# Loading a decayed cumulative sum's first operands by hardware queues as float32 rows, with GpSimd's queue begun later

## The chip, the cores and the metric

The kernel runs on one core of one Trainium2 chip. The metric is device time in microseconds (us). Each version is run several times; one further execution is profiled. Times inside that execution are counted from the start of its span.

The engines are TensorE (PE; PEld is its loading of weights), VectorE (DVE), ScalarE (ACT), GpSimd (POOL) and SyncE (SP). SP, ScalarE and GpSimd can issue DMAs. DMAs issued by SP and ScalarE go through hardware queues, those of GpSimd through a software queue, which alone converts float32 to bfloat16 on the way in this kernel.

## What is computed

```python
B, S, D = 16, 2048, 1024          # x: [B, S, D], w: [D, D], decay: [D], all float32
xw = x @ w
out[:, 0, :] = xw[:, 0, :]
for t in range(1, S):
    out[:, t, :] = decay * out[:, t - 1, :] + xw[:, t, :]
```

## The kernel before, in words

The 16 sequences are cut into 64 chunks of 512 time steps (TL). Chunks go in pairs, so one slot of the main loop is one pair and one of K = 8 blocks n of 128 output columns. For a slot, TensorE runs 8 contraction blocks k for each of the two chunks: 16 matmuls of 128x512, in bfloat16, into PSUM (`matmul`, line 125; the instruction is at line 131). VectorE scans along time, ScalarE copies and scales, GpSimd adds, VectorE transposes back, SP stores.

In the steady state x comes through GpSimd's queue as bfloat16 (`load`, line 101; issued at line 105), VectorE transposes it in 32x32 blocks (`turn`, 115) and ScalarE regroups it into xt (`part`, 123).

The order is written out by hand. `pin` keeps each instruction in program order on its engine, and `agenda` (line 571) is a list of deeds by slot: a letter names a function in `deeds` (line 524), the number is its argument. The list under -99 is the start, before the first slot, and it is the one that changes. Each engine runs its own instructions of that list in order, so a deed that waits holds back every later one on its engine.

What the start has to bring in:

- w comes in four quarters, named (h, e): h is the half of the output columns, e the parity of k. Contraction blocks k = 2m + e, m = 0 to 3, so the quarter (0, 0) holds the even k and (0, 1) the odd k for the first four blocks n. Each quarter is four DMAs, one for each group ("quad") of 32 partitions. `load_w` (321, issued at 323) brings them into `stage`, `settle` (328, copy at 330) rearranges a block of a quarter into `wsb`, which the matmuls read. `settle_slots` (416, copy at 419) does it for some n only: `q4` and `Q4` are the first slot and the others of the block k = 1.
- x's chunk 0 is wanted in two halves of 256 time steps. The first half comes as rows, 128 time steps to a DMA, by SP and ScalarE (line 341), as float32. `gather` (374, copy at 376; deeds H on VectorE, J on ScalarE) casts and regroups it into `upright`, TensorE transposes it against `eye` (`erect`, 383; line 386; deed t) into PSUM (`bed`), and `lay` (389, copy at 393; deeds o on VectorE, O on ScalarE) copies it into xt.
- Chunk 0's second half and chunk 1 come through GpSimd's queue (M1, M2, M3), and VectorE's block transposes (E) and copies (F on VectorE, G on ScalarE) lay them into xt.

TensorE's start is, in order: 12 spins (`spin`, 350; matmuls over zeros, line 352), the transposes t0 to t3, nine spins gated by the landing of w's first quarter (K; `spin_on`, 403, with a small copy on ScalarE at 404), n0 (`begin`, 395: the 16 matmuls over even k of chunk 0's first half, 256 columns each), n1 (the same for its second half), and then, in slot 0 (line 677), the 16 matmuls of 512 columns over the odd k of the whole chunk, followed by chunk 1. These read w's second quarter, settled by q4, w5, Q4, W6 and W7. From there on TensorE goes on into the slots.

GpSimd's start is, in order: U0 (w's first quarter), I1 (`eye`, lines 442 and 443), M1 (x's second half), U1 (w's second quarter), M2 and M3 (chunk 1), U2 and U3 (w's other two quarters).

Of the kernel before, what the change touches and what calls it, by code (L numbers as in the profile page):

```python
# [9 lines left out]
FP32 = mybir.dt.float32  # L10
BF16 = mybir.dt.bfloat16
# [3 lines left out]
def _ap(ap_obj: bass.AP, new_ap, extra_offset=0):  # L15
    return dataclasses.replace(
        ap_obj,
        ap=[list(p) for p in new_ap],
        offset=ap_obj.offset + extra_offset,
    )  # L20
# [5 lines left out]
def kernel(  # L26
# [26 lines left out]
    nc = tc.nc  # L53
    pin = tc.keep_in_program_order
    B, S, D = x.shape
    assert w.shape == (D, D)

    NQ = 4
    P = 32
    CQ = D // NQ  # L60
    K = CQ // P
    M = K // 2
    TL = 512
    NJ = TL // P
# [5 lines left out]
    const = ctx.enter_context(tc.tile_pool(name="const", bufs=1))  # L70
    sb = ctx.enter_context(tc.tile_pool(name="sb", bufs=1))
# [4 lines left out]
    def ring(pool, name, count, shape, dtype=FP32):  # L76
        i = turns[name] = turns.get(name, -1) + 1
        return pool.tile(shape, dtype, name=f"{name}{i % count}")

    def quad(q):  # L80
        return slice(q * P, (q + 1) * P)
# [12 lines left out]
    def ot_tile(nj):  # L94
        return ring(sb, "ot", 4, [128, nj, CR])

    xb_of = {}
    xw_of = {}
    xt_of = {}
# [25 lines left out]
    def matmul(ps, n, k, xt, t0=0, t1=TL, start=0, pairs=None):  # L125
        if pairs is None:
            rhs = xt[:, k // 2, k % 2, t0:t1]
        else:
            rhs = pairs[:, k // 2, t0 // P:t1 // P, :, k % 2].rearrange("p j i -> p (j i)")
        lhs = wsb[:, k, n].rearrange("p q i -> p (q i)")  # L130
        pin(nc.tensor.matmul(  # L131
            out=ps[:, t0:t1] if ps.shape[1] >= t1 else ps,
            lhsT=lhs,
            rhs=rhs,
            start=(k == 0 and t0 == start),
            stop=(k == K - 1),
        ))
# [3 lines left out]
    class Tile:  # L141
# [39 lines left out]
        def copy(self):  # L181
            self.xs = sb.tile([128, 2 * TL], FP32, name=f"xs{self.lot % 3}")[:, 0:self.T]
            parts = self.ps if isinstance(self.ps, tuple) else (self.ps,)
            size = self.T // len(parts)
            for i, ps in enumerate(parts):
                pin(nc.scalar.copy(out=self.xs[:, i * size:(i + 1) * size], in_=ps))  # L186
# [103 lines left out]
    class Outlet:  # L290
# [8 lines left out]
        def store(self, b, t0, j0, j1):  # L299
# [4 lines left out]
            for j in range(j0, j1, nj):  # L304
# [8 lines left out]

    room = [ot_tile(2 * NJ).rearrange("p j c -> p (j c)") for _ in range(2)]
    size = M * CH
    stage = {(0, 0): room[0][:, 0:size // 2].bitcast(BF16),
             (0, 1): room[0][:, size:size * 3 // 2].bitcast(BF16),
             (1, 0): room[1][:, 0:size // 2].bitcast(BF16),
             (1, 1): room[1][:, size // 2:size].bitcast(BF16)}

    def load_w(queues, h, e):
        for i, q in enumerate((0, 2, 1, 3)):
            pin(queues[i % len(queues)].dma_start(  # L323
                out=stage[h, e][quad(q)].rearrange("p (m d) -> p m d", m=M),
                in_=_ap(w, [[2 * D, P], [2 * P * D, M], [1, CH]],
                        (q * CQ + e) * D + h * CH)))
# [6 lines left out]
    idle = const.tile([128, TL], BF16, name="idle")  # L333
    spare = ring(psp, "spare", 1, [128, TL])
    rows = const.tile([128, 2, P], FP32, name="rows")
    touch = const.tile([128, 1], BF16, name="touch")
    H = NJ // 2
    halves = ((0, H), (H, NJ))
    whole = room[1][:, size:2 * size].rearrange("p (u c) -> p u c", u=2)
    for u, queue in enumerate((nc.sync, nc.scalar)):  # L340
        pin(queue.dma_start(out=whole[:, u], in_=_ap(x, [[D, 128], [1, D]], u * 128 * D)))
    pin(nc.vector.memset(idle, 0.0))  # L342
    pin(nc.vector.memset(rows, 0.0))
    pin(nc.scalar.copy(out=touch, in_=idle[:, 0:1]))

    gates = [const.tile([128, 128], BF16, name=f"gate{q}") for q in range(NQ)]
    for gate in gates:
        pin(nc.vector.memset(gate, 0.0))

    def spin(count, by):  # L350
        for _ in range(count):
            pin(nc.tensor.matmul(out=spare, lhsT=by, rhs=idle, start=True, stop=True))  # L352

    spin(12, idle[:, 0:128])
    for q in range(NQ):
        pin(nc.sync.dma_start(
            out=rows[q * P:q * P + R],
            in_=_ap(decay, [[P, R], [CH, 2], [1, P]], q * CR)))
    cols = const.tile([128, 2, P], FP32, name="cols")

    def load_half(i):
# [5 lines left out]
    firsts = [ps[:, 0:TL] for ps in heads] + [spares[0]]  # L367
    seconds = [ps[:, TL:2 * TL] for ps in heads] + [spares[1]]
    eye = const.tile([128, 128], BF16, name="eye")

    upright = room[0][:, size * 3 // 2:2 * size].bitcast(BF16).rearrange(
        "p (e u m c) -> p e u m c", e=2, u=2, m=M)

    def gather(i, copy):
        e, u = i // 2, i % 2
        pin(copy(out=upright[:, e, u].rearrange("p m (q i) -> p m q i", q=NQ),
                 in_=whole[:, u].rearrange(
                     "p (q m i e) -> p e m q i", q=NQ, m=M, e=2)[:, e]))

    def bed(e):  # L380
        return seconds[e].bitcast(BF16).rearrange("p (m t) -> p m t", m=M)

    def erect(i):
        e, u = i // 2, i % 2
        for m in range(M):
            pin(nc.tensor.transpose(
                out=bed(e)[:, m, u * 128:(u + 1) * 128], in_=upright[:, e, u, m], identity=eye))

    def lay(i, copy):
        e, m = i // 2, i % 2 * 2  # L390
        if 0 not in xt_of:
            xt_of[0] = ring(sb, "xt", 5, [128, M, 2, TL], BF16)
        pin(copy(out=xt_of[0][:, m:m + 2, e, 0:H * P], in_=bed(e)[:, m:m + 2]))

    def begin(i):
        for k in range(0, K, 2):
            for n in range(R):
                if i == 0:
                    matmul(firsts[n], n, k, xt_of[0], 0, H * P)
                else:  # L400
                    matmul(firsts[n], n, k, xt_of[0], H * P, TL, pairs=xw_of[0])

    def spin_on(q):
        pin(nc.scalar.copy(out=gates[q][quad(q), 0:1], in_=stage[0, 0][quad(q), 0:1]))
        spin(3 if q == 0 else 2, gates[q])

    def load_part(i):
        load_w((nc.gpsimd,), i // 2, i % 2)

    def part_one(i, copy):  # L410
        part(i // 8, copy, i % 4, i % 4 + 1, *halves[i // 4 % 2])
# [106 lines left out]
    def turn_and_load(c):  # L518
# [16 lines left out]
        "w": lambda i: settle_one(i, nc.scalar.copy),  # L535
        "M": load_half,
        "U": load_part,
        "E": lambda i: turn(i // 8, *halves[i // 4 % 2], i % 4, i % 4 + 1),
        "F": lambda i: part_one(i, nc.vector.tensor_copy),
        "G": lambda i: part_one(i, nc.scalar.copy),  # L540
        "K": spin_on,
        "t": erect,
        "H": lambda i: gather(i, nc.vector.tensor_copy),
        "J": lambda i: gather(i, nc.scalar.copy),
        "O": lambda i: lay(i, nc.scalar.copy),
        "o": lambda i: lay(i, nc.vector.tensor_copy),
        "n": begin,
        "q": lambda i: settle_slots(i, 0, 1),
        "Q": lambda i: settle_slots(i, 1, R),
# [19 lines left out]
        "L": lambda i: load(*loads.pop(0)) if loads else None,  # L569
    }  # L570
    agenda = {
# [92 lines left out]
    for step, (g, n) in enumerate(slots):  # L664
        T = TL * len(g)
        left = step - len(slots)
        if n % R == 0:
            ns, nj = range(n, n + R), T // P
            if left == -2 * R:
                outlets = [Outlet(ns, H, half) for half in range(2)]  # L670
            else:
# [4 lines left out]
        if step == 0:  # L676
# [3 lines left out]
            for k0 in range(0, K, 2):  # L680
                for i in range(R):
                    for k in (k0, k0 + 1):
                        matmul(seconds[i], i, k, xt_of[1], 0, H * P,
                               pairs=xw_of[1] if k0 < 4 else None)
            for i in range(R):
                for k in range(K):
                    matmul(seconds[i], i, k, xt_of[1], H * P, TL, H * P,
                           pairs=xw_of[1] if i < 2 else None)
        if step < R:
            ps = heads[n] if n < 3 else tuple(spares)  # L690
        else:
# [16 lines left out]
            elif step == K:  # L708
                todo = []
                nexts = (ring(psp, "spare", 1, [128, TL]), ring(psp, "ps", 3, [128, TL]))  # L710
                for l in range(len(g)):
                    for i, half in enumerate((ps[:, l * TL:(l + 1) * TL], nexts[l])):
                        for k in range(K):
                            matmul(half, n + i, k, xt_of.get(g[l]),
                                   pairs=xw_of[g[l]] if g[l] in (3,) else None)
# [51 lines left out]
```

## Time and profile before

| what | value |
|---|---|
| median of 3 runs | 903.76 us (903.57 to 903.91) |
| profiled execution: device time | 903.72 us |
| profiled execution: span | 901.9 us |
| granted clock of TensorE, mean | 1.00 |
| TensorE busy in matmuls | 891.2 us, 99% of the span |
| VectorE, ScalarE, GpSimd busy | 91%, 76%, 73% |
| chain that ended last, share on TensorE | 97% |
| w's DMAs, 16 of 128 KB, issue to landing, median | 5.6 us |
| x's first half, two DMAs of 512 KB, issue to landing | 4.7 and 4.9 us |

The span is the time from the first to the last instruction of the profiled execution; the device time is 1.8 us longer. Busy time is a mean over the whole span. The change lies in the first 15 us, so the views that matter are the timelines of the engines there and the chain of waits, not the shares. In a line of a timeline the first number is the start in us, the second the length of the group, then come engine, line, operation, output and input, the count, and in brackets the idle time just before it and what ended it.

### The profile page before, as it was taken

To read this page: it belongs to the slowest core of one execution; us is meant where nothing else is said; L and a number is where in the kernel's file an instruction comes from. 1 tells how busy PE (TensorE), PEld (TensorE's weight loads), DVE (VectorE), ACT (ScalarE), POOL (GpSimd) and SP (SyncE) were. 2 spreads that over 40 slices of the span, in tenths; PEclk is the share of its full clock that TensorE was granted. 3 is DMA by queue.
4 is the path that set the end of the run, shared out by engine and by line. 5 is a ranking of instruction groups with operands and counts; after the bars stand their busy time and mean duration, and the time that the engine had idled before them with its cause. 6 is when DMAs were issued, how large, how long until landed. Compare 5 with 4: busy or idle time off the path is not lost.

```text
span 901.9 us, 12229 instructions
## 1 busy us (share of the span) xinstructions
PE 891.2 (99%) x4131; PEld 411.9 (46%) x4213; DVE 823.5 (91%) x636; ACT 687.1 (76%) x962; POOL 657.2 (73%) x757
## 2 busy tenths in 40 slices
PE   8999999999999999999999999999999999999998
PEld 5544444444444444444444444444444444444444
DVE  4999998989999999999998999999999999999998
ACT  4889867778877877878778778777787787787743
POOL 8888678768767768677677687777777776876532
PEclk9999999999999999999999999999999999999999
DMA  9999999999999999999999999999999999999868
GB/s 193 195 215 218 229 212 207 216 233 247 247 248 255 248 255 252 246 254 250 222 235 228 218 236 227 233 226 227 232 230 227 227 236 222 226 228 221 177 153 231
DMA packets 402382, 204.77 MB, mean 227 GB/s; under 512 B 9360, under 2 KB 401552, under 8 KB 402320
## 3 DMA queue, kind: packets, MB, share of 16 engines
q1 hardware_dynamic: 265664, 134.77, 60.8%
q0 software_dynamic: 136512, 68.70, 56.8%
q8 instruction: 33, 0.54, 0.2%
q10 hardware_dynamic: 144, 0.52, 0.1%
q14 instruction: 29, 0.24, 0.1%
HBM read 138.42 MB, written 134.22 MB: 302 GB/s over the span
## 4 chain that ended last, share of the span: by engine, by line
PE 97%; DMA 1%; issue 1%; POOL 0%; DVE 0%; ACT 0%; DVEq 0%; POOLq 0%
PE ps L131 96%; PE spare L131 1%; DMA ot<-in_w_dram 1%; POOL ot L323 0%; DVE so L233 0%; PE ps L460 0%; PE spare L460 0%; ACT xb L467 0%; DVE wsb L419 0%; DVEq L419 0%; POOLq L751 0%
## 5 line engine op out<-in xcount | busy, mean ns | idle before, releaser
L131 PE MATMUL ps<-xt,wsb 128*128 128x512 bf16 (+1 forms) x3946 | 862.6, 378 | 4.7 <-DVE wsb L419 0.4
L131 PEld LDWEIGHTS <-wsb 128*128 128x128 bf16 x4160 | 406.5, 98 | 479.8 <-issue 0.9
L208 POOL TENSOR_TENSOR xs<-h,xs 128x512 f32<-128x512 f32 (+1 forms) x190 | 242.7, 1278 | 184.1 <-ACT h L169 83.1
L283 DVE STREAM_TRANSPOSE ot<-so 128x1024 f32<-128x1024 f32 (+2 forms) x265 | 300.2, 1171 | 6.5 <-DMA out_dram<-ot 4.4
L186 ACT COPY xs<-ps 128x1024 f32<-128x1024 f32 (+1 forms) x190 | 188.8, 994 | 149.3 <-PE ps L131 137.5
L266 POOL TENSOR_TENSOR so<-h,xs 128x512 f32<-128x512 f32 (+1 forms) x190 | 241.2, 1271 | 46.9 <-ACT h L169 27.2
L123 ACT COPY xt<-xw 128x2048 bf16<-128x2048 bf16 (+1 forms) x133 | 240.6, 1816 | 9.5 <-DVE xw L115 9.5
L105 POOL DMA_DIRECT2D xb<-in_x_dram x260 | 171.6, 661 | 2.9 <-DMA ot<-in_w_dram 0.9
L169 ACT ACTIVATE h<-so,dec 128x512 f32<-128x512 f32 (+1 forms) x190 | 145.3, 766 | 32.8 <-DVE so L213 29.9
L115 DVE STREAM_TRANSPOSE xw<-xb 128x2048 f32<-128x2048 f32 (+1 forms) x74 | 145.9, 1981 | 6.5 <-DMA xb<-in_x_dram 6.5
L213 DVE TENSOR_TENSOR_SCAN so<-spare,keep,xs 128x512 f32<-128x512 f32 (+1 forms) x97 | 119.8, 1237 | 25.9 <-POOL xs L208 25.6
L213 DVE TENSOR_TENSOR_SCAN so<-spare,xs 128x512 f32<-128x512 f32 x93 | 113.0, 1217 | 25.4 <-POOL xs L208 22.8
L169 ACT ACTIVATE h<-ps,dec 128x512 f32<-128x512 f32 (+1 forms) x189 | 129.3, 684 | 0.0
L233 DVE TENSOR_TENSOR_SCAN so<-dec,ps 128x1024 f32<-128x1024 f32 x34 | 76.9, 2260 | 0.8 <-ACT h L169 0.6
L233 DVE TENSOR_TENSOR_SCAN so<-dec,keep,ps 128x1024 f32<-128x1024 f32 (+2 forms) x35 | 74.7, 2138 | 0.0
L270 ACT COPY keep<-so 128x1 f32<-128x1 f32 x136 | 25.2, 188 | 9.1 <-DVE so L233 8.7
L204 ACT COPY so<-keep 128x1 f32<-128x1 f32 x97 | 18.4, 191 | 2.6 <-DVE ot L283 2.4
L131 PE MATMUL spare<-xt,wsb 128*128 128x512 bf16 (+1 forms) x68 | 14.0, 329 | 0.0
L323 POOL DMA_DIRECT2D ot<-in_w_dram x16 | 9.0, 561 | 2.9 <-POOLq L751 0.9
L202 POOL MEMSET so<- 128x1 f32 x93 | 10.7, 116 | 0.6 <-DVE ot L283 0.6
L131 PE MATMUL ps<-xw,wsb 128*128 128x256 bf16 (+1 forms) x56 | 9.3, 307 | 0.8 <-DVE xw L115 0.8
L352 PE MATMUL spare<-idle 128*128 128x512 bf16 x12 | 5.3, 632 | 1.2 <-DVE idle L342 1.2
(46 smaller groups left out, 43.9 us busy)
## 6 DMA issues: line engine op xcount, KB each, us to landing
out_dram<-ot SPq DMA_DIRECT2D x236, 512.0 KB, 10.8
xb<-in_x_dram POOLq DMA_DIRECT2D x248, 256.0 KB, 7.8
out_dram<-ot SPq DMA_DIRECT2D x56, 128.0 KB, 2.5
ot<-in_w_dram POOLq DMA_DIRECT2D x16, 128.0 KB, 5.6
out_dram<-ot SPq DMA_DIRECT2D x8, 256.0 KB, 4.2
xb<-in_x_dram POOLq DMA_DIRECT2D x12, 128.0 KB, 5.3
out_dram<-xb SPq DMA_DIRECT2D x4, 256.0 KB
ot<-in_x_dram ACTq DMA_DIRECT2D x1, 512.0 KB, 4.9
```

The source lines that it names most:

```text
L105: pin(nc.gpsimd.dma_start(out=xb_of[c][quad(q), j0:j1], in_=_ap(x, [[D, P], [P * D, j1 - j0], [1, CQ]], (b * S + t0 + j0 * P) * D + q * CQ)))
L115: pin(nc.vector.transpose(out=dst.rearrange("p (m j i) -> p j m i", m=M, i=P)[:, j0:j1, m0:m1], in_=src.rearrange("p (j m c) -> p j m c", ...
L123: pin(copy(out=xt_of[c][:, m0:m1, :, j0 * P:j1 * P], in_=src))
L131: pin(nc.tensor.matmul(out=ps[:, t0:t1] if ps.shape[1] >= t1 else ps, lhsT=lhs, rhs=rhs, start=(k == 0 and t0 == start), stop=(k == K - 1),))
L169: pin(nc.scalar.activation(out=h, in_=src, func=mybir.ActivationFunctionType.Copy, scale=dec[:, self.n:self.n + 1]))
L186: pin(nc.scalar.copy(out=self.xs[:, i * size:(i + 1) * size], in_=ps))
L208: pin(nc.gpsimd.tensor_tensor(out=odds, in0=self.g, in1=odds, op=ALU.add))
L213: pin(nc.vector.tensor_tensor_scan(out=so[:, 3:T + 2:2], data0=squares[-1][:, n:n + 1].to_broadcast([128, T // 2]), data1=self.xs[:, 1:T:2 ...
L233: pin(nc.vector.tensor_tensor_scan(out=so[:, t + 2:t + 2 + size], data0=dec[:, n:n + 1].to_broadcast([128, size]), data1=ps, initial=befor ...
L266: pin(nc.gpsimd.tensor_tensor(out=self.so[:, 2:T + 2:2], in0=self.h, in1=self.xs[:, 0:T:2], op=ALU.add))
L270: pin(nc.scalar.copy(out=self.keep, in_=self.so[:, self.T + 1:self.T + 2]))
L283: pin(nc.vector.transpose(out=outlet.ot[:, j:j + size, c0:c0 + P], in_=self.so[:, t1:t1 + size * P].rearrange("p (i t) -> p i t", t=P)))
```

## The change

It rewrites the start alone; everything from slot 0 on stays as it is.

- w's first quarter is loaded as float32 by SP (quads 0 and 1) and ScalarE (quads 2 and 3), behind x's first half on the same two queues. Its room in `stage` doubles, and `upright` moves into chunk 0's buffer of xw, which is not needed otherwise any more. `settle` of this quarter casts from float32 now.
- x's second half comes as rows too, one DMA on SP and one on ScalarE behind w's first quarter, into the buffer of xb that chunk 0 used. It takes the road of the first half: gathers H4, J5, H6, J7, transposes t4 to t7, copies o4, O5, o6, O7. The DVE transposes E4 to E7 and the copies G4, G5, F6, G7 go. `begin` is cut in four: n0 and n1 are the first half with k = 0, 2 and k = 4, 6; n2 and n3 the second half.
- GpSimd's queue begins with w's second quarter (U1). Ahead of it stands a new deed `v` (`hold`), a copy of two columns of x's first half, which waits until that has landed. U0 and M1 are gone.
- The four gates, their memsets and their copies on ScalarE go; K7 is seven spins without a gate, and m3 three spins into another bank, behind n1.
- Of w's first quarter VectorE settles blocks 0 and 1 and ScalarE blocks 2 and 3 (before: VectorE 0, 1 and 3, ScalarE 2).

```diff
--- before.py
+++ after.py
@@ -313,14 +313,14 @@
 
     room = [ot_tile(2 * NJ).rearrange("p j c -> p (j c)") for _ in range(2)]
     size = M * CH
-    stage = {(0, 0): room[0][:, 0:size // 2].bitcast(BF16),
+    stage = {(0, 0): room[0][:, 0:size],
              (0, 1): room[0][:, size:size * 3 // 2].bitcast(BF16),
              (1, 0): room[1][:, 0:size // 2].bitcast(BF16),
              (1, 1): room[1][:, size // 2:size].bitcast(BF16)}
 
-    def load_w(queues, h, e):
-        for i, q in enumerate((0, 2, 1, 3)):
-            pin(queues[i % len(queues)].dma_start(
+    def load_w(queue, h, e, quads):
+        for q in quads:
+            pin(queue.dma_start(
                 out=stage[h, e][quad(q)].rearrange("p (m d) -> p m d", m=M),
                 in_=_ap(w, [[2 * D, P], [2 * P * D, M], [1, CH]],
                         (q * CQ + e) * D + h * CH)))
@@ -334,24 +334,35 @@
     spare = ring(psp, "spare", 1, [128, TL])
     rows = const.tile([128, 2, P], FP32, name="rows")
     touch = const.tile([128, 1], BF16, name="touch")
+    held = const.tile([128, 2], FP32, name="held")
     H = NJ // 2
     halves = ((0, H), (H, NJ))
-    whole = room[1][:, size:2 * size].rearrange("p (u c) -> p u c", u=2)
-    for u, queue in enumerate((nc.sync, nc.scalar)):
-        pin(queue.dma_start(out=whole[:, u], in_=_ap(x, [[D, 128], [1, D]], u * 128 * D)))
+    xb_of[0] = ring(sb, "xb", 3, [128, NJ, CQ], BF16)
+    xw_of[0] = ring(sb, "xw", 2, [128, M, NJ, P, 2], BF16)
+    wholes = [room[1][:, size:2 * size],
+              xb_of[0].rearrange("p j c -> p (j c)").bitcast(FP32)]
+    wholes = [half.rearrange("p (u c) -> p u c", u=2) for half in wholes]
+
+    def load_rows(queue, i, u):
+        pin(queue.dma_start(
+            out=wholes[i][:, u], in_=_ap(x, [[D, 128], [1, D]], (2 * i + u) * 128 * D)))
+
+    load_rows(nc.sync, 0, 0)
+    load_rows(nc.scalar, 0, 1)
+    load_w(nc.sync, 0, 0, (0, 1))
+    load_w(nc.scalar, 0, 0, (2, 3))
+    load_rows(nc.sync, 1, 0)
+    load_rows(nc.scalar, 1, 1)
     pin(nc.vector.memset(idle, 0.0))
     pin(nc.vector.memset(rows, 0.0))
     pin(nc.scalar.copy(out=touch, in_=idle[:, 0:1]))
 
-    gates = [const.tile([128, 128], BF16, name=f"gate{q}") for q in range(NQ)]
-    for gate in gates:
-        pin(nc.vector.memset(gate, 0.0))
-
-    def spin(count, by):
+    def spin(count, into=spare):
         for _ in range(count):
-            pin(nc.tensor.matmul(out=spare, lhsT=by, rhs=idle, start=True, stop=True))
-
-    spin(12, idle[:, 0:128])
+            pin(nc.tensor.matmul(
+                out=into, lhsT=idle[:, 0:128], rhs=idle, start=True, stop=True))
+
+    spin(12)
     for q in range(NQ):
         pin(nc.sync.dma_start(
             out=rows[q * P:q * P + R],
@@ -368,44 +379,43 @@
     seconds = [ps[:, TL:2 * TL] for ps in heads] + [spares[1]]
     eye = const.tile([128, 128], BF16, name="eye")
 
-    upright = room[0][:, size * 3 // 2:2 * size].bitcast(BF16).rearrange(
-        "p (e u m c) -> p e u m c", e=2, u=2, m=M)
+    upright = xw_of[0].rearrange("p m j i e -> p (m j i e)").rearrange(
+        "p (h e u m c) -> p h e u m c", h=2, e=2, u=2, m=M)
 
     def gather(i, copy):
-        e, u = i // 2, i % 2
-        pin(copy(out=upright[:, e, u].rearrange("p m (q i) -> p m q i", q=NQ),
-                 in_=whole[:, u].rearrange(
+        h, e, u = i // 4, i // 2 % 2, i % 2
+        pin(copy(out=upright[:, h, e, u].rearrange("p m (q i) -> p m q i", q=NQ),
+                 in_=wholes[h][:, u].rearrange(
                      "p (q m i e) -> p e m q i", q=NQ, m=M, e=2)[:, e]))
 
-    def bed(e):
-        return seconds[e].bitcast(BF16).rearrange("p (m t) -> p m t", m=M)
+    def bed(h, e):
+        return seconds[2 * h + e].bitcast(BF16).rearrange("p (m t) -> p m t", m=M)
 
     def erect(i):
-        e, u = i // 2, i % 2
+        h, e, u = i // 4, i // 2 % 2, i % 2
         for m in range(M):
             pin(nc.tensor.transpose(
-                out=bed(e)[:, m, u * 128:(u + 1) * 128], in_=upright[:, e, u, m], identity=eye))
+                out=bed(h, e)[:, m, u * 128:(u + 1) * 128],
+                in_=upright[:, h, e, u, m], identity=eye))
 
     def lay(i, copy):
-        e, m = i // 2, i % 2 * 2
+        h, e, m = i // 4, i // 2 % 2, i % 2 * 2
         if 0 not in xt_of:
             xt_of[0] = ring(sb, "xt", 5, [128, M, 2, TL], BF16)
-        pin(copy(out=xt_of[0][:, m:m + 2, e, 0:H * P], in_=bed(e)[:, m:m + 2]))
+        pin(copy(out=xt_of[0][:, m:m + 2, e, h * H * P:(h + 1) * H * P],
+                 in_=bed(h, e)[:, m:m + 2]))
 
     def begin(i):
-        for k in range(0, K, 2):
+        h, k0 = i // 2, i % 2 * M
+        for k in (k0, k0 + 2):
             for n in range(R):
-                if i == 0:
-                    matmul(firsts[n], n, k, xt_of[0], 0, H * P)
-                else:
-                    matmul(firsts[n], n, k, xt_of[0], H * P, TL, pairs=xw_of[0])
-
-    def spin_on(q):
-        pin(nc.scalar.copy(out=gates[q][quad(q), 0:1], in_=stage[0, 0][quad(q), 0:1]))
-        spin(3 if q == 0 else 2, gates[q])
+                matmul(firsts[n], n, k, xt_of[0], h * H * P, (h + 1) * H * P)
+
+    def hold(i):
+        pin(nc.gpsimd.tensor_copy(out=held, in_=wholes[0][:, :, 0:1].rearrange("p u c -> p (u c)")))
 
     def load_part(i):
-        load_w((nc.gpsimd,), i // 2, i % 2)
+        load_w(nc.gpsimd, i // 2, i % 2, (0, 2, 1, 3))
 
     def part_one(i, copy):
         part(i // 8, copy, i % 4, i % 4 + 1, *halves[i // 4 % 2])
@@ -538,7 +548,9 @@
         "E": lambda i: turn(i // 8, *halves[i // 4 % 2], i % 4, i % 4 + 1),
         "F": lambda i: part_one(i, nc.vector.tensor_copy),
         "G": lambda i: part_one(i, nc.scalar.copy),
-        "K": spin_on,
+        "K": spin,
+        "m": lambda i: spin(i, seconds[0]),
+        "v": hold,
         "t": erect,
         "H": lambda i: gather(i, nc.vector.tensor_copy),
         "J": lambda i: gather(i, nc.scalar.copy),
@@ -569,7 +581,7 @@
         "L": lambda i: load(*loads.pop(0)) if loads else None,
     }
     agenda = {
-        -99: "U0 I1 M1 U1 M2 M3 U2 U3 H0 J1 t0 t1 H2 J3 t2 t3 O1 o0 K0 O3 o2 K2 K1 K3 W0 W1 w2 W3 n0 E4 E5 G4 E6 G5 E7 F6 G7 n1 q4 w5 Q4 W6 W7 D E8 E9 G8 E10 G9 E11 F10 G11 E12 L E13 G12 L E14 G13 E15 L F14 G15",
+        -99: "I1 v U1 M2 M3 U2 U3 H0 J1 t0 t1 H2 J3 t2 t3 O1 o0 O3 o2 K7 W0 w2 W1 w3 n0 n1 H4 J5 m3 H6 J7 t4 t5 o4 O5 n2 t6 t7 o6 O7 n3 q4 w5 Q4 W6 W7 D E8 E9 G8 E10 G9 E11 F10 G11 E12 L E13 G12 L E14 G13 E15 L F14 G15",
```

## The prediction, made before the changed kernel ran

> **What bounds the kernel now.** I read the waits of TensorE first, then the chain that ended last, then the timeline of each engine over the first 30 us, then the DMA queues in the same stretch. Waits of TensorE from 15 us to 898 us:
>
> ```profile
> engine line waited for: us in total, times, longest us
> PE ps L131 <- DVE wsb L419: 0.4, 1, 0.4
> ```
>
> That one wait ends at 14.97 us. Behind it TensorE never waits for another engine until the tail near 897 us, so the span is the moment T1 at which the matmuls over odd k of chunk 0 begin, plus a fixed run of matmuls: 901.9 - 14.97 = 886.9 us, with nothing in it that the change touches. An edit is worth what it does to T1, as long as what comes behind T1 is still fed. The chain of waits from 0 to 30 us says who sets T1 (start, length, what):
>
> ```profile
> 1.31 1.25 POOL ot L323 x2
> 2.56 5.65 DMA ot<-in_w_dram
> ...
> 9.16 5.43 DMA ot<-in_w_dram
> ...
> 14.72 0.21 DVE wsb L419
> ...
> 14.97 0.39 PE ps L131
> ```
>
> The last piece of w's second quarter is issued at 9.16 and lands at 14.60; VectorE copies a slot of it (0.21) and TensorE starts. T1 is bound by GpSimd's queue, whose third issue of that quarter had waited for a landing at 8.21. The timeline of TensorE shows what stands ahead of T1:
>
> ```profile
> 1.20 5.30 PE L352 MATMUL spare<-idle 128*128 128x512 bf16 x12 [1.20 <-DVE idle L342]
> 6.29 1.34 PE L386 MATMUL ps<-eye,ot 128*128 128x128 bf16 x16
> 7.95 2.16 PE L352 MATMUL spare<-idle,gate 128*128 128x512 bf16 x9 [0.32 <-ACT gate L404]
> ...
> 12.62 0.51 PE L131 MATMUL ps<-xw,wsb 128*128 128x256 bf16 x3 [0.76 <-DVE xw L115]
> ...
> 14.97 0.82 PE L131 MATMUL ps<-xt,wsb 128*128 128x512 bf16 x2 [0.37 <-DVE wsb L419]
> ```
>
> The 12 opening spins start 0.43 us apart; the spins from 7.95 start 0.22 apart: until about 7.0 us the array runs at half its later pace (the granted clock reads 1.00 in each of these stages; the spacing of the starts tells it). The second half of x is waited for at 12.62 (0.76 idle). The copies between, from the timelines of VectorE and ScalarE:
>
> ```profile
> 7.84 0.98 DVE L393 COPY xt<-ps 128x512 bf16<-128x512 bf16 x2 [1.62 <-ACT xt L393]
> 9.00 0.70 DVE L330 COPY wsb<-ot 128x512 bf16<-128x512 bf16 x3 [0.17 <-DMA ot<-in_w_dram]
> ```
>
> **The change, part by part.** Times are in this profiled execution (span 901.9, device time 903.72, 0.04 under the median of 903.76).
>
> *Loads.* w's first quarter goes as 1.05 MB of float32 (before: 0.52 MB, cast by GpSimd's queue), and x's second half as 1.05 MB of rows, both behind x's first half on the SP and ScalarE queues. The DMA queues over the first 5 us (packets, MB, share):
>
> ```profile
> q1 hardware_dynamic: 143, 0.52, 34.5%
> q10 hardware_dynamic: 133, 0.52, 26.7%
> q0 software_dynamic: 7, 0.01, 1.3%
> ```
>
> All of x's first half is moved by 5.0 us, at 367 to 451 GB/s in each half microsecond from 3.0 on, and GpSimd's queue, issuing since 1.31, had got 0.01 MB. It landed at 5.43 and 5.65, so some 0.5 after its bytes. I take 410 GB/s for what follows: w's quarter 5.0 + 2.55, landed at 8.1; x's second half 2.55 more, landed at 10.6 (A). The eight issues cost 0.4 each (rows of 0.39 and 0.41); on ScalarE three more push its table load (1.28) from 1.18 to 2.4, inside the 2.98 that it idles before 5.65; on SP the decay loads come about 1.2 later and are first read at 15.47. Nothing for both.
>
> *GpSimd.* It loses eight issues (first quarter and x's second half) and gets a copy of 128x2 that waits for x's first half. No row has it; between a memset of 128x1 (0.12) and an add of 128x512 (1.28) I take 0.2, by the nearer. Queued behind it are all of GpSimd's loads. The second quarter is then issued from 5.8 to 8.1 (four of 0.56); before it was 6.88 to 9.8. At 5.0 to 6.0 from issue to landing (that line's own range) the last lands at 13.1 (12.5 to 13.5): T1 could be 13.5 by this road, 1.5 earlier, and the stall at 14.97 goes. By bytes it is the same: 3.15 MB after 5.0, the last third at the software queue's 193 GB/s of written bytes, give 12.8 and the landing. Chunk 1's halves, w's third and fourth quarter follow at the 2.7 us each that they take now, so each lands 1.5 or more earlier than now; nothing behind T1 starves. What is late next is TensorE's own program order.
>
> *TensorE up to T1.* Spins and the first 16 transposes stay: held by the spins until 6.29, not by x. Seven ungated spins of 0.22 instead of nine gated ones: done at 9.1. The first matmuls need w's first block. VectorE ends its second copy into xt at 8.82, so it starts that block at 8.84, with w landed since 8.1 (0.7 of cover; beyond it, each microsecond of lateness is one in T1). The block is now a cast from float32: between the bf16 copy (0.29) and the float32 gather of line 376, same shape (0.43 to 0.46), I take 0.43, as it is the same cast. So:
>
> - first matmul at 9.27 + 0.06 (the wait at 12.62 came 0.06 after its transpose) = 9.33; before 9.95, a gain of 0.6
> - 16 matmuls of 256 columns at 0.109: 11.07
> - three spins of 0.22 (m3): 11.72. x's second half is there by 10.6 and gathered by 11.35 (0.43, 0.65), so nothing waits for it
> - eight transposes at 0.056 (a quarter of a 512-column spin): 12.17
> - a copy out of PSUM before the next matmul: 0.13 + 0.42 + 0.06 (latency from 7.15 to 7.23 above, drain, then the 0.42 of line 393): 12.78. This idle is new
> - eight matmuls, eight transposes, eight matmuls: 0.87 + 0.45 + 0.87: T1 = 14.97.
>
> Beside it: the last transposes end at 14.1, VectorE copies until 14.65 and settles the first slot of the second quarter (0.20) until 14.85: just in time. ScalarE's copy waits for that of VectorE on the same bank (as at 7.84), until 15.25, then settles block w5 (0.62) until 15.87, needed at 15.84: 0.1 of stall. Effective T1 is **15.07, 0.1 later than now**: the queue's 1.5 is real, but 16 more transposes (0.9), three spins (0.65) and the new round trip (0.6) take the place of 0.76 and 0.37 of idle. VectorE loses four transposes and a copy (1.8 us) and ScalarE three (1.7); neither had been what T1 waited for.
>
> The sum: 903.72 + 0.1 = **903.8 us**.
>
> The Trainium skill bears on the loads. Its page "DMA: Bandwidth & Descriptors", section "Issuing engines are not separate DMA queues", says that DMAs of all issuers share the same 16 engines and interleave, and that several issuers save only issue time. That speaks against an earlier x: its second half would share with GpSimd's queue (second rival). With equal shares the sum would be 905.5 (worked out there from rows), without sharing it is the 903.8 above. The first 5 us (0.01 MB for GpSimd) don't show sharing, but they can't exclude that its descriptors simply came late.
>
> **Rivals.**
> 1. *The clock opens earlier.* The pace doubled at about 7.0 in this execution, by the spacing of the matmuls. Today's T1 hangs on a DMA and doesn't care; the new T1 hangs on TensorE's order. If the pace doubles at 5, spins and transposes end 0.7 sooner, until A binds: second gather 11.35, transposes 11.6, copy, 2.2 of matmuls and transposes: T1 = 14.4, 903.1. If it doubles at 8, T1 is 0.25 later. One profile can't say which is usual. The skill's page "TensorE: Matmul & The Clock Gate" (Part 1) agrees with the spacing: half rate until one free-running window of 3.4 us was busy, so the point varies.
> 2. *x's second half comes late* (slower). Place: the two hardware rings while GpSimd's second quarter runs beside them, from about 7. Price: from A on, gather 0.66, one transpose group 0.28, copy 0.61, then 2.2 make T1 = A + 3.75, which decides from A = 11.3. With equal shares, x and w together end at 12.6, A = 13.0, T1 = 16.75: 905.5. With a fifth for GpSimd, A is 11.1 and nothing happens. The same follows if w's first quarter, in pieces of 32 partitions, moves at the 193 GB/s of the software queue: it lands at 10.6, T1 at about 16.9: 905.7. For it: no row has such pieces on a hardware queue, and the DMA share is above 1 whenever GpSimd's queue moves data. Against: the first 5 us.
> 3. *The pace falls back* after idle of 0.6 and more just before T1. The matmuls after the 0.76 of idle at 12.62 ran at 0.109, so it would need far more; a fall for some 4 us costs 2: 906.
> 4. *It does nothing that counts*: w's second quarter still lands at 14.6, because bytes and not issues limit it: T1 again 14.97, 903.7.
>
> **How the numbers follow.** Forecast and rival 4 together 0.6 (903.7 to 904.1), rival 1 on its early side 0.2 (903.1 to 903.6), rival 2 0.16 (904.2 to 905.7, a third of it over 905.5), rival 3 0.03, a gain that I don't see 0.01. The range, 902.9 to 905.3, leaves out about 0.1. A difference of 0.2% is 1.8 us, about what a measurement of this kernel can tell from no change; the whole start can hardly yield that, as T1 would have to be 13.2, where TensorE's own order from 9.1 on already needs 5.0. So faster 0.02, same 0.90, slower 0.08.
>
> **What would show it.** Right: no wait of TensorE for a settled slot of w; second quarter landed near 13; first matmul near 9.3; one idle of about 0.6 near 12.5, released by the copy out of PSUM; odd k from about 15. Wrong: a gather that waits for a DMA after 11.3 (rival 2), transposes 0.056 apart before 6.5 (rival 1), matmuls of 256 columns 0.2 apart after 12 (rival 3), or any wait of TensorE between 16 and 890 us, which would mean that the run behind T1 isn't fixed.

## The result, and the profile after

The changed kernel takes **905.26 us** (904.91 to 905.75, 18 runs), the kernel before 903.71 (903.28 to 904.11, 18 runs): ratio 1.0017, 95% interval 1.0009 to 1.0024. That is 1.55 us more, where 0.1 was forecast. The profiled execution has a span of 903.5 and took 905.27.

Waits of TensorE in the whole span:

```profile
engine line waited for: us in total, times, longest us
PE spare L362 <- DVE idle L356: 1.2, 1, 1.2
PE ps L131 <- ACT wsb L330: 1.1, 1, 1.1
PE ps L397 <- DVE xw L387: 0.9, 1, 0.9
PE ps L131 <- DVE xt L405: 0.5, 1, 0.5
PE ps L131 <- ACT xt L405: 0.2, 1, 0.2
```

The wait for a slot of w's second quarter is gone, as forecast. In its place stand a wait for the first settled blocks of w's first quarter (1.1; the list names ScalarE's cast, but VectorE's ended at the same 10.17, and the first matmuls read VectorE's blocks) and two for the copies out of PSUM (0.5 and 0.2). The 0.9 is early slack: the opening spins ended sooner here. The timeline of TensorE places them:

```profile
10.23 0.50 PE L131 MATMUL ps<-xt,wsb 128*128 128x256 bf16 x3 [1.12 <-ACT wsb L330]
...
12.63 0.61 PE L397 MATMUL ps<-eye,xw 128*128 128x128 bf16 x8
13.76 0.38 PE L131 MATMUL ps<-xt,wsb 128*128 128x256 bf16 x2 [0.51 <-DVE xt L405]
14.37 0.27 PE L131 MATMUL ps<-xt,wsb 128*128 128x256 bf16 x1 [0.24 <-ACT xt L405]
...
16.34 0.81 PE L131 MATMUL ps<-xt,wsb 128*128 128x512 bf16 x3
```

T1 is 16.34 instead of 14.97, 1.37 later. Behind it w5 costs 0.09 (the fifth of these matmuls starts 0.95 after the first instead of 0.86), and from there to the last copy the two traces run 1.46 to 1.47 apart: nothing in between gives or takes anything. The last 0.13 of the 1.6 in the spans lies behind that copy, in the final store.

The timelines of ScalarE and VectorE show the first block (line 330 settles w; CAST, since w is float32 now), and the DMA issues of the first 5 us how long each load took to land (KB each, us from issue):

```profile
9.55 0.62 ACT L330 CAST wsb<-ot 128x512 bf16<-128x512 f32 x1 [1.34 <-DMA ot<-in_w_dram]
9.59 0.58 DVE L330 CAST wsb<-ot 128x512 bf16<-128x512 f32 x1 [0.92 <-DMA ot<-in_w_dram]
```

```profile
ot<-in_w_dram ACTq DMA_DIRECT2D x2, 256.0 KB, 7.7
ot<-in_w_dram SPq DMA_DIRECT2D x2, 256.0 KB, 6.9
xb<-in_x_dram SPq DMA_DIRECT2D x1, 512.0 KB, 8.8
xb<-in_x_dram ACTq DMA_DIRECT2D x1, 512.0 KB, 9.5
```

Issued at 1.66, 2.12 and 2.15, these land at 8.55 on SP and 9.35 on ScalarE for w, and at 10.9 and 11.6 for x's second half. Forecast were 8.1 and 10.6.

### The profile page after: what moved, and what is told of

Its sections match the earlier page's. It is cut to its first block, busy times and chain, and to the rows that moved or that the text cites. A ratio compares the mean times of both kernels' runs of the same rounds, so it can differ in the third digit from the quotient of the medians.

```text
span 903.5 us, 12254 instructions
## 1 busy us (share of the span) xinstructions
PE 891.3 (99%) x4147; PEld 412.6 (46%) x4230; DVE 824.7 (91%) x630; ACT 688.1 (76%) x960; POOL 653.8 (72%) x750
## 4 chain that ended last, share of the span: by engine, by line
PE 97%; DMA 2%; issue 1%; POOL 0%; DVE 0%; ACT 0%; DVEq 0%
PE ps L131 96%; PE spare L131 1%; DMA ot<-in_w_dram 1%; DMA ot<-in_x_dram 1%; DMA xb<-in_x_dram 1%; POOL xb L105 0%; DVE so L233 0%; PE ps L470 0%; DVE xw L115 0%; PE spare L470 0%; ACT xb L477 0%; POOL held L415 0%; DVEq L115 0%
## 5 line engine op out<-in xcount | busy, mean ns | idle before, releaser
L105 POOL DMA_DIRECT2D xb<-in_x_dram x256 | 169.7, 664 | 3.7 <-DMA ot<-in_w_dram 2.1
L131 PE MATMUL spare<-xt,wsb 128*128 128x256 bf16 (+1 forms) x71 | 14.7, 325 | 0.0
L323 POOL DMA_DIRECT2D ot<-in_w_dram x12 | 6.7, 561 | 1.3 <-issue 0.6
L131 PE MATMUL ps<-xw,wsb 128*128 128x256 bf16 (+1 forms) x44 | 7.4, 315 | 0.1
```

The costliest lines, as they stand in the source:

```text
L105: pin(nc.gpsimd.dma_start(out=xb_of[c][quad(q), j0:j1], in_=_ap(x, [[D, P], [P * D, j1 - j0], [1, CQ]], (b * S + t0 + j0 * P) * D + q * CQ)))
L131: pin(nc.tensor.matmul(out=ps[:, t0:t1] if ps.shape[1] >= t1 else ps, lhsT=lhs, rhs=rhs, start=(k == 0 and t0 == start), stop=(k == K - 1),))
```

## The experiments

The kernel before ran beside each of them, with medians of 903.70 to 903.82. Theory 1: the loss is TensorE's own chain up to T1, made of a late w, a wait on a PSUM tile, and the longer road of x. Each edit is against the changed kernel.

**n2_last**

```diff
-        for k in (k0, k0 + 2):
-            for n in range(R):
-                matmul(firsts[n], n, k, ...)
+        some = [(n, k) for k in (k0, k0 + 2) for n in range(R)]
+        if i == 2:
+            some.sort(key=lambda nk: nk[0] == 2)
```

> The changed kernel with one reordering: in n2 the two matmuls of n = 2 go last (they wrote into the bank pair whose other bank ScalarE was still copying from, and the first of them started at 14.37, right at that copy's end at 14.33, after 0.24 us of idle on top of the 0.14 lost before). Theory 1 (the loss is TensorE's own chain up to T1: w 0.9 late, this wait 0.39, the rest as forecast): T1 from 16.34 to about 15.95, the time from 905.26 to about 904.9. Rival (VectorE's chain, the copies of the second transposes and q4, ends last anyway): T1 stays, 905.3.

Measured: 904.71. T1 is 15.81, with no wait on ScalarE's copy:

```profile
13.62 0.38 PE L131 MATMUL ps<-xt,wsb 128*128 128x256 bf16 x2 [0.52 <-DVE xt L405]
13.83 0.27 PE L131 MATMUL spare<-xt,wsb 128*128 128x256 bf16 x1
```

From the start of n2 to T1 it is 2.19 (before the edit 16.34 - 13.76 = 2.58): the 0.39, as theory 1 has it. The other 0.14 of the 0.53 was won ahead of n2: the first matmul started at 10.09. n = 2 writes one bank of a tile of two, while ScalarE copies from the other. Whether only the program's bookkeeping by tiles asks for that wait was not tried.

**no_m3**: `m3` taken out of the agenda.

> The changed kernel without the three spins m3. Theory 1: the transposes t4 start at 12.0 instead of 12.63, t5 is then held by ScalarE's gather (ends 12.25), so the copy out of PSUM starts 0.5 earlier (12.75), T1 about 15.85, the time about 904.8. Rival (the spins keep the pace up): matmuls of 256 columns 0.2 apart instead of 0.109 after the idle, T1 later, 906 or more. Rival (x's second half binds): unchanged, 905.3.

Measured: 904.72, T1 15.89. Here t5 waits for ScalarE's gather (0.15) as expected, and matmuls stay 0.109 apart: the spins m3 kept up no pace that would have been lost. They only stood in the way. Of the 0.45 in T1, 0.18 was won ahead of them (first matmul at 10.05 instead of 10.23), so 0.27 is what their removal gave.

**w_by_half**

```diff
-    load_w(nc.sync, 0, 0, (0, 1))
-    load_w(nc.scalar, 0, 0, (2, 3))
+    for m in (0, 2):
+        for queue, quads in ((nc.sync, (0, 1)), (nc.scalar, (2, 3))):
+            for q in quads:
+                pin(queue.dma_start(out=... [:, m:m + 2], in_=...))
```

> The changed kernel with each DMA of w's first quarter cut in two along m, all quads' m = 0, 1 ahead of all quads' m = 2, 3: eight DMAs of 128 KB for four of 256 KB, two more issues of 0.42 to 0.45 on each of the two queues. The first blocks then need half the bytes. Theory 1: first blocks landed by about 8.0, VectorE settles from 8.7 on, the first matmul at 9.3 to 9.4 instead of 10.23. But x's second half lands at 10.9 and 11.65, gathered by 12.25, so t5 waits and only about 0.3 to 0.4 of the 0.9 comes through: 904.9. If the whole 0.9 comes through: 904.4. Rival (w is not what TensorE waits for): 905.3.

Measured: 908.62; all expectations missed. The edit has a cost of its own: ScalarE issued its fifth DMA at 5.97, just when the first had landed, and the sixth at 7.03. Its table load, which stands behind them, came at 7.41, the second transpose group waited 2.9 us for ScalarE's gather, and the granted clock was 0.50 from 9 to 15 us. It tells nothing of w's form.

**no_hold**: `v` taken out of the agenda.

> The changed kernel without the copy that holds GpSimd's queue back, so w's second quarter is issued from about 1.4 on. Theory 1 (the hardware queues' traffic is served ahead, GpSimd's queue moved nothing before 10 us in the changed kernel and 0.01 MB before 5 us in the kernel before): x's second half lands as now, within 0.3, T1 unchanged, 905.2. Rival (equal shares between the queues): w's first quarter and x's second half each 1 to 2 us later, T1 up by 1 or more, 906 to 907.

Measured: 907.78 (two runs near 906.3, three near 907.8; rows_alone, below, comes back to the two groups). Theory 1's claim, that the hardware queues are served ahead, fell: with GpSimd's loads issued from 1.5 us on, its queue took 20 to 35% of the DMA engines' time from 6 to 11 us, w's last piece lands at 10.4, one microsecond later, x's second half 1.4 later (12.3 and 13.05), and T1 is 17.28 in the profiled execution, one of the shorter ones. So the queues share. In the changed kernel the hold keeps them apart: GpSimd's queue moved nothing before 10 us there. That queue also starts late while the hardware queues are full: its first bytes moved at 5.7, some 4 us after the first issue (1.52); in x2_late, below, with the hardware queues nearly drained, 1.4 us after (6.38 to 7.8).

The Trainium skill, page "DMA: Bandwidth & Descriptors", section "Issuing engines are not separate DMA queues", had said that they interleave; this run agrees, with its 1.0 us.

**chain_short**: no m3, `t6 t7` ahead of n2, n2 as in n2_last, gathers `H4 H6 H5 J7`.

> The changed kernel with TensorE's chain ahead of T1 shortened and its loads left alone: no m3, the transposes t6 and t7 moved ahead of n2 (into the wait for the copy o4), n = 2 last in n2, and three of the four gathers of x's second half on VectorE. Theory 1 (TensorE's program order and its waits set T1): t5 at 12.15, copy 12.6 to 13.0, then n2 and n3 without a gap, T1 about 14.8 to 15.0, the time 903.6 to 903.9, the whole loss gone. Rival (w's second quarter ends last, whose last piece lands at 13.75 in the changed kernel): T1 not below 14.2, the same here, but a wait of TensorE or of VectorE for that piece would stand in the trace. Rival (the loss has another part behind T1): 904.3 or more.

Measured: 903.83 (before beside it 903.80; ratio 0.9998, 0.9989 to 1.0007). With w landing no earlier (first matmul 10.16) the whole loss is gone, T1 is 14.88 and TensorE's list of waits has, behind its first instruction, one entry for the whole span:

```profile
PE ps L131 <- DVE wsb L330: 1.1, 1, 1.1
```

w's second quarter ends its own road just ahead: VectorE waits 0.5 for it until 14.03. From the first matmul to T1 it is 4.72 now, 6.11 in the changed kernel: TensorE's order, with one gather moved from ScalarE to VectorE, can give the whole loss back though w still lands late. That doesn't make the order its only source: w_rows, below, gives most of it back with w's form alone. There was no other part behind T1.

**x2_late**: x's second half issued by ScalarE behind w3 (one run).

> The changed kernel with x's second half issued only after ScalarE has settled w's first quarter, so that nothing stands behind that quarter on the hardware queues. Theory 1 (the last engines to finish w's quarter are held up by bytes of x's second half that run ahead on the others and on the SP queue): w's last piece lands near 8.4 instead of 9.35, the first matmul at about 9.4. Rival (pieces of 32 partitions and 2 KB rows are slow by themselves): it lands at 9.0 or later, as now. The time itself is worse, x coming 2 us later: 907 or more.

Measured: 913.68, and w's last piece lands at 9.0. Of the 1.25 us between forecast (8.1) and fact (9.35), the bytes queued behind w thus explain at least 0.35. The run isn't a clean one: GpSimd's queue began at 7.8 here, beside the end of w, while in the changed kernel it moved nothing before 10. How much of the rest is the pieces themselves is read from w_rows and pairs.

**w_alone**: x's second half by GpSimd's queue as before (`I1 M1 U1`, `E4` to `G7`), no hold, no m3.

> Half of the change: w's first quarter by the hardware queues as float32; x's second half by GpSimd's queue and VectorE's block transposes as before, first in that queue, then w's second quarter; no hold, no m3. Theory 1 (what the change pays for is the second road of x through TensorE): no added transposes and round trip; x's second half issued from 1.5, served behind the hardware queues, lands by about 10, w's second quarter about 12.8, T1 about 13.5 to 14.5, the time 902.3 to 903.3, faster than before. Rival (the queues share, as without the hold): w's first quarter lands about 10 and x about 12, T1 about 15, 903.8 or more.

Measured: 903.87; the rival is right. TensorE waits for w's first quarter until 10.76 and for its second until 15.01:

```profile
10.76 0.50 PE L131 MATMUL ps<-xt,wsb 128*128 128x256 bf16 x3 [1.50 <-DVE wsb L330]
...
15.01 0.82 PE L131 MATMUL ps<-xt,wsb 128*128 128x512 bf16 x3 [0.38 <-DVE wsb L428]
```

That is the kernel before's T1 (14.97). The last line there has the same wait as before the change: the same 4.2 MB of x and w must be in, and here it made no difference to T1 that the hardware queues issued w's first quarter.

**rows_alone**: w's first quarter by GpSimd's queue from the start, x's second half as rows by hardware (`U0 I1 U1`).

> The other half: x's second half as rows by the hardware queues behind the first, w's first quarter by GpSimd's queue from the start as before, then w's second quarter, no hold. Theory 1 (GpSimd's queue is served behind the hardware queues): x lands by about 8.5, w's first quarter about 10.5, the first matmul at about 11, the chain as in the changed kernel (6.1 to T1): T1 about 17, the time 905.9. Rival (w's first quarter loses nothing): first matmul at 9.9, T1 about 15.9, 904.7.

Measured: 907.82 (two runs near 906.2, four from 907.7 to 908.4). The first matmul is at 11.47, nearer to theory 1, but TensorE had idled for 2.7 us, and in the profiled execution, one of the longer ones, the granted clock (the number before DMA share and GB/s at the end of the line) falls:

```profile
12.00:13.00 1.00, 1.00 (x9) 0.82 (x8) 0.33 (x1) 1.00 (x3) 1.00 (x3) 0.75 1.23 196
13.00:14.00 1.00, 1.00 (x7) 0.69 (x5) 0.00 (x0) 0.34 (x1) 0.90 (x3) 0.50 1.41 186
```

It stays at 0.50 until nearly 16, and T1 is 19.26. The two groups of runs, here and in no_hold, would be those with and without such a fall; of neither kernel were both groups profiled. The mean granted clock on record for each run agrees: 0.998 in all seven longer runs of the two kernels, 0.999 to 1.000 in the four shorter ones. A fall to 0.50 for 3.5 us would take 0.5 * 3.5 / 904 = 0.002 off the mean (an estimate from rows_alone's profile). The figure alone doesn't prove it: one run of the kernel before, at 904.53, has 0.997. What decides in which executions the clock falls is not shown.

**w_rows**

```diff
-    load_w(nc.sync, 0, 0, (0, 1))
-    load_w(nc.scalar, 0, 0, (2, 3))
+    for u, queue in enumerate((nc.sync, nc.scalar)):
+        pin(queue.dma_start(
+            out=stage[0, 0][:, u * D:(u + 1) * D],
+            in_=_ap(w, [[D, 128], [1, D]], u * 128 * D)))
```

> The changed kernel with w's first quarter replaced by as many bytes in another form: two DMAs of 128 whole rows of w (128 partitions, 4 KB rows, 512 KB each) instead of four of 32 partitions and 2 KB rows. The matmuls over even k then use the wrong weights; times are what is looked at. Theory 1a (the form makes w late: 367 to 381 GB/s and engines that finish apart): the two land near 8.0 to 8.5 instead of 8.55 and 9.35, the first matmul at 9.3 to 9.5, T1 up to 0.4 earlier, since x's second half then binds: 904.8 to 905.0. Rival (bytes and the depth of the two queues alone): landed at 8.9 or later on ScalarE's queue, T1 within 0.15, 905.2.

**pairs**: `load_w(nc.sync, 0, 0, (0, 2))` and `load_w(nc.scalar, 0, 0, (1, 3))`.

> The changed kernel with the quads paired the other way: quads 0 and 2 on SP, 1 and 3 on ScalarE, so that the first pieces of the two queues, moving side by side, go to partitions 0 to 63 instead of 0 to 31 and 64 to 95. Theory 1a (the form of the pieces counts, by which partitions are written at once): w's last piece lands 0.5 or more later than 9.35 and the time is up by as much, 905.7 or more. Rival (only bytes count): landed within 0.2 of 9.35, time 905.2.

Measured: 904.14 for w_rows (ratio to the kernel before 1.0003, 0.9992 to 1.0015), 906.71 for pairs. The same bytes in three forms, in the stretch in which they move (the last number is GB/s; the changed kernel, pairs, w_rows):

```profile
6.00:7.00 1.00, 0.76 (x11) 0.59 (x12) 0.46 (x2) 1.00 (x2) 0.73 (x2) 1.00 1.06 367
```

```profile
6.00:7.00 1.00, 1.00 (x11) 0.70 (x10) 0.50 (x2) 0.96 (x2) 0.93 (x2) 1.00 0.97 201
```

```profile
6.00:7.00 1.00, 1.00 (x16) 0.82 (x15) 0.24 (x1) 1.00 (x3) 0.81 (x2) 1.00 1.07 442
```

Whole rows over 128 partitions move at 402 to 442 GB/s and land at 7.9 and 8.3; pieces of 32 partitions that go to 0 to 31 and 64 to 95 side by side, at 344 to 381, landed at 9.35; the same pieces side by side in partitions 0 to 63, at 201 to 320 while w moves, landed at 11.1. (One of the five runs of pairs took 908.24, with a mean clock of 0.998; the others had 1.000.) With whole rows the first matmul starts at 8.83, without a wait, and T1 is 14.95. Its timeline:

```profile
8.83 0.50 PE L131 MATMUL ps<-xt,wsb 128*128 128x256 bf16 x3
...
14.95 0.81 PE L131 MATMUL ps<-xt,wsb 128*128 128x512 bf16 x3
```

Theory 1a holds: the form made w late, by 1.1 us. T1 gained even more than expected (1.4), since x's second half came earlier too (10.5 and 10.6). Pairs changes nothing but which partitions are filled side by side, so that effect is shown by itself. w_rows changes three things at once, the partitions of a piece, the length of a row (4 KB for 2) and the number of DMAs (two for four); which of them makes whole rows faster than the changed kernel's pieces was not separated.

**w_full** (on chain_short): w's first quarter by blocks, `out=stage[0, 0][:, m * CH:(m + 1) * CH]`, `in_=_ap(w, [[CQ * D, NQ], [2 * D, P], [1, CH]], 2 * P * m * D)`. **w_rows_short**: chain_short with the loads of w_rows.

> chain_short with w's first quarter in four DMAs over all 128 partitions, one for each block m (256 KB, 2 KB rows, two on each hardware queue; each goes through the four groups of 32 rows of w as its outermost loop). Same data as before. Theory 1a (partitions written at once decide): w lands at about 8.2 as with whole rows, first matmul at 8.8, T1 set by x's second half or by w's second quarter at about 14.1, the time 902.9 to 903.2, faster than both kernels. Rival: the Trainium skill, page DMA: Bandwidth & Descriptors, section on why a DMA increments its semaphore by 16, says that a DMA runs on at most as many engines as divide the outermost sizes of both sides, here 4 of 16; then a quarter of the rate, w beyond 13, the pace of TensorE lost in the idle, the time 909 or more.

> chain_short together with the replaced form of w's first quarter (two DMAs of 128 whole rows; wrong weights for even k): how much of the start can be had if neither the form of w's pieces nor TensorE's order is in the way. Theory 1: w at 8.2, x's second half at 10.3 and 10.6, copies at 11.6, T1 would be 13.9 by TensorE's order; w's second quarter, last piece issued near 8.0 and landed near 13.6, settled 0.37 later, makes it 14.0: the time 902.9 to 903.1. Rival (something behind T1 takes it back): 903.7.

Measured: 919.1 for w_full; 903.38 for w_rows_short (ratio 0.9996, 0.9986 to 1.0006). In w_full the first blocks of w were there at 15.95 and the last after 23 us. From 15 to 17 us, when little else moved, the rate was 82 to 86 GB/s, and the mean busy share of the 16 DMA engines (the number ahead of it) 0.28, as much as 4 to 5 engines:

```profile
15.00:16.00 1.00, 0.00 (x0) 0.00 (x0) 0.05 (x1) 0.00 (x0) 0.00 (x0) 0.50 0.28 86
```

Of that, 0.01 to 0.02 MB per us was still GpSimd's queue. That is the rival: the Trainium skill's page "DMA: Bandwidth & Descriptors", section "Why a DMA increments its semaphore by 16 and not by 1", lets such a DMA run on 4 of 16 engines, and a rate near a fifth of 410 agrees. It says nothing against the effect of partitions, which it could not reach. In w_rows_short, T1 is 14.50 (for 14.0 expected; the time, too, is above the 902.9 to 903.1 expected), bound by w's second quarter, which landed at 14.1 and not at 13.6:

```profile
14.25 0.36 DVE L433 COPY wsb<-ot 128x128 bf16<-128x128 bf16 x2 [1.26 <-DMA ot<-in_w_dram]
```

With both faults away the start wins 0.47 in T1 and 0.3 in time, which the interval can't tell from no change. Then w's second quarter is the bound again, settled from 14.25 on instead of 14.72 in the kernel before. From 10 us on GpSimd's queue moved alone there, at 138 to 182 GB/s; whether the bytes ahead of it or that queue's own pace sets the 14.25 was not separated.

**All together.** Median device time less T1 of the one profiled execution, for the kernels with a steady clock: before 888.74, changed 888.92, n2_last 888.90, no_m3 888.83, chain_short 888.95, w_alone 888.86, pairs 888.86, w_rows_short 888.88; w_rows is 0.3 above. T1 alone explains times from 903.4 to 906.7 within 0.2, that one apart.

## Why the prediction was right and where it was wrong

The time lies in the forecast range of 902.9 to 905.3, but at its upper edge, and "same", the likeliest class, came true by its bound of 0.2% (measured 0.17%); the interval (1.0009 to 1.0024) shows a real, small slowdown. The middle was off by 1.4 us: 905.26 lies outside the band that had 0.6, and in the one of rival 2 (0.16). Of that rival's two reasons the late x didn't set T1; the other, w late by the form of its pieces, came in part. That the range held, by 0.04, is in part luck: two steps of the sum were wrong.

- *T1 plus a fixed run* (right): see the differences above.
- *"What is late next is TensorE's own program order"* (right): chain_short touches none of the loads (it takes m3 away, moves transposes and n = 2, and gives one gather to VectorE) and takes the loss back.
- *w's second quarter* (right in kind): its stall is gone; its last piece landed at 13.75 for 13.1 forecast, still hidden.
- **"I take 410 GB/s for what follows: w's quarter 5.0 + 2.55, landed at 8.1"**: this step failed. The rate came from rows over 128 partitions, and w's pieces cover 32. They landed at 9.35 (w_rows: 8.3). "0.7 of cover" was used up, and the first matmul came at 10.23 instead of 9.33. Of these 0.90, 0.51 are the landing beyond the 8.84 at which VectorE was to start, 0.24 go from the landing to its start at 9.59, and 0.15 are the cast, taken at 0.43 from the gather and measured at 0.58. Rival 2 had named the form of the pieces, at a price for half the rate; the rate was 0.84 to 0.93 of the one assumed. That alone would make w some 0.3 us later (an estimate from 2.55 us at 410 GB/s). The two queues also shared unevenly: from 5 to 8 us SP's moved 0.61 MB and ScalarE's 0.51, and it was ScalarE's pieces that landed last. How the rest splits is open.
- **"eight matmuls, eight transposes, eight matmuls"**: a wait was missing in it. n = 2 shares its tile with the bank that ScalarE copies from: 0.39 (n2_last).
- *The idle for the copy out of PSUM*: forecast 0.61, and 3.45 from first matmul to n2; measured 3.53. *w5*: forecast 0.1, measured 0.09. The sum of what failed, 0.90 + 0.39 + 0.08 = 1.37, is T1's shift.
- *Rival 2, shares*: in the changed kernel GpSimd's queue moved nothing before 10 us, by the hold; no_hold shows that sharing costs 1 us for w. The forecast had the right landing order for the wrong reason: I read the 0.01 MB of the first 5 us as the queue being served behind the others, but its first bytes came some 4 us after its first issue in no_hold (1.52 to 5.7), in rows_alone (1.31 to 5.5) and in the changed kernel (6.43 to about 10.4), and once they moved, the queues shared.
- *Rival 2, the late x*: its sign came (x's second half landed at 11.6, past 11.3, and ScalarE's gather waited for it), but by its own sum, 11.6 + 3.75, T1 would have been near 15.4. It was not what bound T1 at 16.34; only without m3 did a transpose wait for it, 0.15.
- *Rival 1, the pace*: it opened at about 4.1 us in the changed kernel's profiled execution, but w came late, so nothing of it reached T1.

## What to carry to other kernels

Where a DMA bounds the start, work out first whether bytes or issue order hold it: here the last of the same 4.2 MB of x and w landed between 13.6 and 14.6 us in eight kernels that shared them out differently between the queues (before, changed, no_hold, chain_short, w_alone, rows_alone, w_rows, w_rows_short; pairs was later, at 15.5), and in no_hold issuing w's second quarter 5 us earlier left it at 14.0. Take a rate only from a row with the same partitions and row length. When a stall ahead of a fixed run goes, price everything that then stands in the bound engine's own order, each wait on a shared PSUM tile among it, and fill the latency of a copy with work that doesn't need it (t6 and t7 ahead of n2, with m3 away, n = 2 last and one gather moved to VectorE, gave back 1.4 us).

## What the runs showed of the hardware, not expected

- Two hardware queues filling 32-partition pieces side by side: 344 to 381 GB/s with partitions 0 to 31 and 64 to 95 and then 32 to 63 and 96 to 127, 201 to 320 with 0 to 63 and then 64 to 127; whole rows over 128 partitions, twice as long and in half as many DMAs, 402 to 442.
- A DMA over 128 partitions whose source has an outermost loop of 4: 82 to 86 GB/s, at a DMA share of 0.28 (w_full).
- 2.7 to 2.9 us without a matmul could halve the granted clock (rows_alone, w_by_half), and the fall can come after work has begun again: in rows_alone work resumed at 11.47, and the clock fell within the stretch from 12 to 13 us, to come back only near 16. In pairs' profiled execution 2.53 us without one did not.
- With four large DMAs outstanding, SP and ScalarE issued a fifth only when the first had landed (w_by_half 5.72 and 5.97; in the changed kernel SP's decay loads at 5.98); ScalarE's compute instructions behind it wait too (its table load at 7.41). Size counts as well as number: behind three large ones, two of 1 KB still went at once (x2_late 2.76, w_alone 2.84) and the next waited (5.90 and 6.07). Whether the hardware or the program's own semaphores hold them is open.
